# Storing split projection weights in the mixer's first block, and moving one PSUM copy from VectorE to ScalarE

## The chip, the cores and the metric

The kernel runs on one core of one Trainium2 chip. The metric is the device time of one execution in microseconds; three runs of the kernel before gave 3564.45, 3571.49 and 3570.65 us, median 3570.65. Engines are named as in the profile: PE is TensorE, DVE is VectorE, ACT is ScalarE, POOL is GpSimd, SP is SyncE. On SP only DMA issues run in this kernel, and all DMAs of it are issued there.

## The reference: what is computed

One encoder layer over 2048 tokens of width 1024: a hybrid token mixer (half mLSTM with 4 heads, half RWKV7 with 8 heads), cross attention to 256 memory rows, and a gated FFN with a short convolution. The change lies in the mixer. What it computes, shortened:

```python
def hybrid_token_mixer(h, w_in, ...):
    p = h @ w_in                       # 1024 x 3880 columns
    pm, pr = p[..., :M_COLS], p[..., M_COLS:]
    qk = silu(causal_dwconv(pm[..., :2 * M_WIDTH], m_conv_w, m_conv_b))
    hm = mlstm_chunkwise(q, k, v, i_pre, f_pre)
    y_m = sigmoid(o) * standardize_heads(hm) * m_norm_g
    pr = token_shift(pr, r_mu)
    ...
    yr = rwkv7_scan(rr, w, kr, vr, kk, a)
    ...
    return concatenate([y_m, y_r], -1) @ w_out

def rwkv7_scan(r, w, k, v, kk, a):
    def step(state, inp):
        sk = einsum('bhvk,bhk->bhv', state, kk_t)
        state = (state * w_t[:, :, None, :] - sk[..., None] * (kk_t * a_t)[:, :, None, :]
                 + v_t[..., None] * k_t[:, :, None, :])
        return state, einsum('bhvk,bhk->bhv', state, r_t)
```

All of it is in float32, and the result is compared with the float32 reference.

## The kernel before

**Split matmuls.** A float32 matrix product is made of three matmuls in the type fp32r: a number is split into a high part (a cast to fp32r) and a low part (the number minus its high part), and hi·hi + hi·lo + lo·hi are accumulated. An activation tile `hA` (128 x 2 x 512) holds both parts of 128 features by 512 tokens. A weight (128 output columns by 1024 inputs, 512 KB) is loaded as one tile `wraw` (`load_raw`, line 96; two buffers) and split in two halves q = 0, 1 of four 128x128 tiles each: ACT casts (`whi`, line 101), POOL subtracts (`wlo`, line 105; in the mixer every twelfth on DVE). `whi` and `wlo` have four buffers each, two weights. A projection (`proj`, `dense_g`, line 122) is 24 matmuls of 128x128 by 512.

**The mixer** goes over the tokens in four blocks of 512. In each block the stream `st_dense` makes 31 projections with the 31 weight groups of `w_in`: number 14 first, then 12 and 13 (`block_front`), then in turn three for a pair of RWKV heads (`f`) and four for an mLSTM head (`q`, in `qkvo`). So each of the 31 weights is loaded and split once a block, four times in all (124 loads of `wraw<-w_in`). At a block's begin `norm_block` builds the eight `hA` tiles: DVE scales (362), ACT casts (363), and line 364 subtracts for the low part, on DVE where k is odd and on POOL where it is even. `hA` has eight buffers, one block. `proj` of number 14 takes the low parts of the activations last (`late`).

**The other streams** of the mixer: `rwkv_pre` prepares a pair of heads and stores blocks of its triangular matrices (`nd<-F`, line 642), `rwkv_solve` inverts 16x16 blocks on DVE after a round trip through DRAM (656, 676, 678), `rwkv_merge` joins them, `rwkv_seq` goes through the eight chunks of 64 tokens in order, and `rwkv_tail`, `gates`, `mlstm` and `mlstm_tail` do the rest. `norm_stats` loads the next block's tokens (`xtok`).

**One chunk of `rwkv_seq`**, which the change touches: PE makes `qy` from state and `UV`; after LQ (1241 ns of planned time) ACT copies `qy` to `q` (747), ACT scales the old state to `sp` (749), PE multiplies the solved matrix with `q` into `pu`; the 64 solved rows are copied from PSUM into `UV` (755, on DVE); after LU (178 ns) PE makes `pS` from `UV`, DVE the new state `sbd` (761), PE the chunk's output, which ACT copies to `yt` (768). There are 16 pairs of heads and blocks with eight chunks each, 128 in all.

**What sets the order.** Each stream is a Python generator; `run_streams` interleaves them by a planned clock that counts PE time alone and the latencies (LQ, LU, ...) given after each step, with the fixed priority seq, gates, tail, merge, ml, pre, dense. That gives the order in which instructions are written. The framework's scheduler then sets each engine's queue from that order, by its own simulation, buffers included; every engine works through its queue in order. After the four blocks `kv_prep` makes the attention's folded key and value weights, and then attention and FFN follow, which use `load_w` too (w_out, f_up).

Of the kernel before, what the change touches and what calls it, by code (L numbers as in the profile page):

```python
# [56 lines left out]
def tile_hybrid_encoder(ctx: ExitStack, tc: tile.TileContext, t_in: dict, out: bass.AP, stage: str = "all"):  # L57
# [50 lines left out]
    wld = [12]  # L108
    wn = [0]

    def load_w(src):
        raw = load_raw(src)
        return [split_w(raw[:, 4 * q:4 * q + 4, :], [P, 4, P], wpool, ("whi", "wlo"), WB) for q in range(2)]

    pe = [0.0]
    DG = 1
# [126 lines left out]
    def mixer():  # L243
# [36 lines left out]
        LB, LPW, LPA, LSS, LPB, LKR, LPV = 3718, 2651, 17094, 3221, 2104, 1813, 344  # L280
        LF, LG, LGD, LQK, LFD, LME, LM1 = 1590, 0, 1147, 3611, 844, 676, 3063
        LM2, LM3, LM4, LMD, LSOLVE = 2779, 438, 1685, 295, 39163
        LATE, PRB, HD, TSB = True, 2, 1, 6
        PMG = PM

        def norm_stats(tok0):
# [61 lines left out]
        def norm_block(tok0, st):  # L348
            rs, xs = st
            bc = PD(name="bc")  # L350
            for j in range(4):
                mm(bc[:, j * P:(j + 1) * P], rs[:, j:j + 1].to_broadcast([P, P]), ident, start=True, stop=True)
            yield LB
            hs = []
            for k in range(KT):
                h = kt.tile([P, 2, TB], FR, tag="kt", name="hA")
                if xs:
                    xr = xs[k]
                else:
                    xr = T(name="xraw")  # L360
                    nc.sync.dma_start(xr, t_in["xT"][k * P:(k + 1) * P, tok0:tok0 + TB])
                nc.vector.scalar_tensor_tensor(xr, xr, V("norm_mix", k), bc, ALU.mult, ALU.mult)
                nc.scalar.copy(h[:, 0, :], xr)  # L363
                (nc.vector if k % 2 and (xs or HD) else nc.gpsimd).tensor_tensor(h[:, 1, :], xr, h[:, 0, :].bitcast(F32), ALU.subtract)
                hs.append(h)
            return hs

        w14 = load_w(t_in["w_in"][14])
        rs = norm_stats_first()


# [358 lines left out]
        def rwkv_seq(d):  # L730
            j, pc = d["j"], d["pc"]
            yt = TS((P, 4, P), "yt")
            for cg in range(NC_):
                sd_, c = d["subs"][cg // 4], cg % 4
                KR, F, UV = sd_["KR"], sd_["F"], sd_["UV"]
                sb, sn = sbd[j][scount[j] % 2], sbd[j][(scount[j] + 1) % 2]
                scount[j] += 1
                qy = PY((P, P), "qy")
                mm(qy, KR[:, c, :], sb, start=True, stop=False, skip_group_check=True)
                for h in range(2):  # L740
                    hs = slice(h * 64, h * 64 + 64)
                    g = 2 * c + h
                    mm(qy[0:66, hs], F[:, g * 130:g * 130 + 66], UV[:, c, hs], start=False, stop=True,
                                     skip_group_check=True)
                yield LQ
                q = sm.tile([P, P], F32, name="q")
                nc.scalar.copy(q, qy)
                sp = sm.tile([P, P], F32, name="sp")
                nc.scalar.activation(sp, sb, AF.Copy, scale=pc[:, cg:cg + 1])
                pu = PU((P, P), "pu")  # L750
                for h in range(2):
                    hs = slice(h * 64, h * 64 + 64)
                    g = 2 * c + h
                    mm(pu[0:66, hs], sd_["R"][:, g * 64:g * 64 + 66], q[:, hs], start=True, stop=True)
                nc.vector.tensor_copy(UV[0:64, c, :], pu[0:64])
                yield LU
                pS = PU((P, P), "pS")
                mm(pS, sd_["et"][c // 2][:, c % 2, :], UV[:, c, :], start=True, stop=True)
                for h in range(2):
                    hs = slice(h * 64, h * 64 + 64)  # L760
                    nc.vector.scalar_tensor_tensor(sn[hs, hs], pS[hs, hs], pc[hs, cg:cg + 1], sp[hs, hs], ALU.mult, ALU.add)
                for h in range(2):
                    hs = slice(h * 64, h * 64 + 64)
                    g = 2 * c + h
                    mm(qy[:, hs], F[:, g * 130 + 2:g * 130 + 130], UV[:, c, hs], start=False, stop=True,
                                     skip_group_check=True)
                o = (cg % 2) * 64
                nc.scalar.copy(yt[o:o + 64, cg // 2, :], qy[64:128])
                if c == 3:
                    yield ("set", "seq_sub")  # L770
                yield LS
            return yt
# [152 lines left out]
        def block_front(blk, w14, rs):  # L925
            h_ = hraw if U0 and blk == 0 else (yield from norm_block(blk * TB, rs))
            x14 = shift((yield from proj(w14, h_, LATE)), 14)
            s1f = x14[0:32]
            nc.scalar.activation(s1f, s1f, AF.Tanh, scale=0.5)
            nc.vector.tensor_scalar(s1f, s1f, 0.5, 0.5, ALU.mult, ALU.add)  # L930
            s1 = lp.tile([96, TB], FR, name="sg1", bufs=2)
            nc.scalar.copy(s1[0:32], s1f)
            nc.scalar.copy(s1[64:96], s1f)
            nc.vector.tensor_tensor(s1[32:64], s1f, s1[0:32].bitcast(F32), ALU.subtract)
            bks[blk] = dict(h=h_, x14=x14, tok0=blk * TB)
            yield ("set", ("x14", blk))
            x12 = shift((yield from proj(load_w(t_in["w_in"][12]), h_)), 12)
            thf = x12[0:64]
            nc.scalar.activation(thf, thf, AF.Tanh)
            tw_ = lp.tile([P, TB], FR, name="tw_")  # L940
            nc.scalar.copy(tw_[0:64], thf)
            nc.vector.tensor_tensor(tw_[64:128], thf, tw_[0:64].bitcast(F32), ALU.subtract)
            ta_ = lp.tile([P, TB], FR, name="ta_")
            nc.scalar.copy(ta_[64:128], x12[64:128])
            nc.vector.tensor_tensor(ta_[0:64], x12[64:128], ta_[64:128].bitcast(F32), ALU.subtract)
            x13 = shift((yield from proj(load_w(t_in["w_in"][13]), h_)), 13)
            sg0 = lp.tile([P, TB], F32, name="sg0", bufs=2)
            nc.scalar.activation(sg0, x13, AF.Tanh, scale=0.5)
            nc.vector.tensor_scalar(sg0, sg0, 0.5, 0.5, ALU.mult, ALU.add)
            bks[blk]["lora"] = (tw_, ta_, sg0, s1)  # L950

        def qkvo(bk, h):
            q2 = conv_qk((yield from proj(load_w(t_in["w_in"][15 + 4 * h]), bk["h"], conv=True)), h)
            k2 = conv_qk((yield from proj(load_w(t_in["w_in"][16 + 4 * h]), bk["h"], conv=True)), 4 + h)
            xv = TM(name="mv")
            nc.scalar.copy(xv, (yield from proj(load_w(t_in["w_in"][17 + 4 * h]), bk["h"], conv=True)))
            og = TM(name="og")
            nc.scalar.activation(og, (yield from proj(load_w(t_in["w_in"][18 + 4 * h]), bk["h"], conv=True)), AF.Tanh, scale=0.5)
            nc.vector.tensor_scalar(og, og, 1.0, mngh[:, h:h + 1], ALU.add, ALU.mult)
            return q2, k2, xv, og  # L960

# [4 lines left out]
        def st_dense():  # L966
            rs_ = rs
            for b in range(NBLK):
                if b == 0:
                    yield from block_front(b, w14, rs_)  # L970
                else:
                    yield from block_front(b, load_w(t_in["w_in"][14]), rs_)
                if b + 1 < NBLK:
                    rs_ = norm_stats((b + 1) * TB)
                nf, nq = 4 * b, 4 * b
                for what in (DL if b + 1 == NBLK else DO):
                    if what == "f":
                        i, j, nf = nf, nf % 4, nf + 1
                        if i > 0:
                            yield ("wait", ("pre", i - 1) if W1 == 0 else ("presub", i - 1, 1), 0)  # L980
                        xs = []
                        for which in range(3):
                            xs.append(shift((yield from proj(load_w(t_in["w_in"][3 * j + which]), bks[b]["h"])), which * 4 + j))
                        fr[i] = xs
                        yield ("set", ("fd", i))
                    else:
                        i, j, nq = nq, nq % 4, nq + 1
                        if i > 0:
                            yield ("wait", ("ml_mid" if W2 < 2 else "pht", i - 1), 0)
                            if W2 == 0:  # L990
                                yield ("wait", ("pht", i - 2), 0)
                        qk[i] = yield from qkvo(bks[b], j)
                        yield ("set", ("qk", i))
# [487 lines left out]
```

## Time and profile before

| | before |
|---|---|
| median of 3 runs | 3570.65 us (3564.45 to 3571.49) |
| the profiled execution | 3564.44 us, span 3562.6 us |
| granted PE clock, mean | 0.981 |
| busy: PE, DVE, ACT, POOL | 3377.6, 2020.6, 1256.2, 1368.7 us |
| `whi` casts (line 101), all | 383.4 us in 596 |
| `wlo` subtractions on POOL (line 105), all | 785.7 us in 544 |
| DMA | 342.01 MB, mean 96 GB/s |

How its lines are read: a group of instructions names line, engine, operation, output and inputs, the count, then busy time and mean ns of one, then the engine's idle time just before them with what ended it. A line of waits names who waited, for whom, the total in us, how often, and the longest. A row of stretches gives for each engine its busy time and, in brackets, its instructions. "min/median/max" rows give durations in ns. Waits are inferred from semaphores; idle time of an engine that does not set the end costs nothing.

### The profile page before, as it was taken

The page shows a single profiled execution, that of the slowest core. Times are in us where ns is not written, and L with a number is a line of the kernel's source. Part 1 is how long each engine was busy: PE and PEld are TensorE (multiplying, and loading weights), DVE is VectorE, ACT ScalarE, POOL GpSimd, SP SyncE. Part 2 cuts the span into 40 slices and gives each one's busy share as a digit, 9 for nine tenths or more (in the row PEclk, how much of TensorE's full clock was granted, in tenths as well). Part 3 has the DMA queues.
Part 4 walks back from the last instruction along what each step waited for, and adds up shares of the span by engine and source line. Part 5 has one row for each costly group of instructions (what it writes and reads, how often), then busy time and mean ns, then how long its engine had stood idle before and what let it go on. Part 6 is the DMA issues. An engine that isn't in the chain of part 4 may idle for free.

```text
span 3562.6 us, 48272 instructions
## 1 busy us (share of the span) xinstructions
PE 3377.6 (95%) x17836; PEld 2750.2 (77%) x17836; DVE 2020.6 (57%) x4038; ACT 1256.2 (35%) x2397; POOL 1368.7 (38%) x1364
## 2 busy tenths in 40 slices
PE   7999999999989999789999999999999999999997
PEld 5777777777767778668888888888788888888886
DVE  6788888878888887433333343444453344344345
ACT  5345434544454444433222212212442222222213
POOL 5233333433333322353144434434632343443433
PEclk9999999999999999899999999999999999999998
DMA  4223222322222234685621111112566411111111
GB/s 131 80 67 111 77 72 75 111 70 68 90 73 69 73 94 146 212 269 177 222 71 43 59 42 54 54 36 71 154 219 212 141 55 36 54 54 42 54 48 54
DMA packets 203388, 342.01 MB, mean 96 GB/s; under 512 B 77072, under 2 KB 108944, under 8 KB 203152
## 3 DMA queue, kind: packets, MB, share of 16 engines
q1 hardware_dynamic: 203152, 338.92, 30.2%
q8 instruction: 141, 2.31, 0.3%
q14 instruction: 95, 0.78, 0.1%
HBM read 293.68 MB, written 45.15 MB: 95 GB/s over the span
## 4 chain that ended last, share of the span: by engine, by line
PE 55%; DMA 4%; DVE 2%; ACT 1%; issue 0%; POOL 0%; SPq 0%; DVEq 0%; ACTq 0%; POOLq 0%
PE pd L148 11%; PE pd L151 11%; PE pd L150 11%; PE dps L1354 4%; PE dps L1352 4%; PE dps L1353 4%; DMA x<-xT 2%; PE sc L1233 1%; PE sc L1235 1%; PE sc L1234 1%; DVE x L1369 0%; DMA wqk<-qk_dram 0%; PE ppt L1258 0%; DVE x L1201 0%; DMA y<-y_dram 0%
## 5 line engine op out<-in xcount | busy, mean ns | idle before, releaser
L105 POOL TENSOR_TENSOR wlo<-wraw,whi 128x512 fp32r<-128x512 f32 (+1 forms) x544 | 785.7, 1451 | 813.0 <-ACT whi L101 736.3
L122 PE MATMUL pd<-hA,whi 128*128 128x512 f32 x1984 | 677.6, 415 | 11.2 <-ACT uconv L824 5.8
L101 ACT CAST whi<-wraw 128x512 fp32r<-128x512 f32 (+1 forms) x596 | 383.4, 651 | 540.9 <-PE pd L150 222.0
L151 PE MATMUL pd<-h,wlo 128*128 128x512 f32 x1408 | 547.9, 389 | 0.0
L148 PE MATMUL pd<-h,whi 128*128 128x512 f32 x1408 | 547.9, 389 | 0.0
L150 PE MATMUL pd<-h,whi 128*128 128x512 f32 x1408 | 547.7, 389 | 0.0
L122 PEld LDWEIGHTS pd<-hA,whi 128*128 128x128 f32 x1984 | 357.5, 191 | 80.4 <-ACT hA L363 8.3
L122 PE MATMUL pd<-hA,wlo 128*128 128x512 f32 x992 | 402.2, 405 | 0.0
L1355 DVE TENSOR_TENSOR x<-dps,x 128x512 f32<-128x512 f32 x352 | 235.5, 689 | 224.3 <-PE dps L1354 222.2
L150 PEld LDWEIGHTS pd<-h,whi 128*128 128x128 f32 x1408 | 264.3, 188 | 54.8
L151 PEld LDWEIGHTS pd<-h,wlo 128*128 128x128 f32 x1408 | 264.3, 188 | 54.8
L148 PEld LDWEIGHTS pd<-h,whi 128*128 128x128 f32 x1408 | 264.3, 188 | 54.7
L1354 PE MATMUL dps<-act,wlo 128*128 128x512 f32 x704 | 271.5, 390 | 0.0
L1353 PE MATMUL dps<-act,whi 128*128 128x512 f32 x704 | 271.4, 390 | 0.0
L1352 PE MATMUL dps<-act,whi 128*128 128x512 f32 x704 | 261.6, 390 | 3.2 <-DVE x L1355 2.6
L122 PEld LDWEIGHTS pd<-hA,wlo 128*128 128x128 f32 x992 | 189.8, 191 | 34.2 <-issue 0.7
L1336 DVE SCALAR_TENSOR_TENSOR fu<-fu,pd 128x512 f32<-128x512 f32 x88 | 60.5, 688 | 226.6 <-PE pd L151 221.7
L1155 POOL TENSOR_TENSOR sq<-sq 128x512 f32<-128x512 f32 x56 | 73.9, 1320 | 252.9 <-ACT sq L1152 231.5
L1352 PEld LDWEIGHTS dps<-act,whi 128*128 128x128 f32 x704 | 132.6, 188 | 31.9 <-DVE x L1355 3.4
L1354 PEld LDWEIGHTS dps<-act,wlo 128*128 128x128 f32 x704 | 132.6, 188 | 27.6
L1353 PEld LDWEIGHTS dps<-act,whi 128*128 128x128 f32 x704 | 132.4, 188 | 27.5
L1330 POOL TENSOR_TENSOR fu<-fu,bcs 128x512 f32<-128x512 f32 x88 | 114.2, 1298 | 97.1 <-DVE fu L1329 95.6
(913 smaller groups left out, 6220.2 us busy)
## 6 DMA issues: line engine op xcount, KB each, us to landing
wraw<-w_in SPq DMA_DIRECT2D x124, 512.0 KB, 3.5
wraw<-f_up SPq DMA_DIRECT2D x88, 512.0 KB, 3.4
wqk<-qk_dram SPq DMA_DIRECT2D x64, 512.0 KB, 5.3
wvo<-vo_dram SPq DMA_DIRECT2D x64, 512.0 KB, 4.2
wraw<-f_down SPq DMA_DIRECT2D x44, 512.0 KB, 3.4
wraw<-w_out SPq DMA_DIRECT2D x32, 512.0 KB, 5.6
y<-y_dram SPq DMA_DIRECT2D x32, 256.0 KB, 7.0
x<-xT SPq DMA_DIRECT2D x32, 256.0 KB, 5.1
```

What stands on the lines that cost most here:

```text
L101: nc.scalar.copy(hi, raw)
L105: (nc.vector if dve else nc.gpsimd).tensor_tensor(lo, raw, hi.bitcast(F32), ALU.subtract)
L122: nc.tensor.matmul(out_, lhsT, rhs, **kw)
L148: nc.tensor.matmul(ps, hi[:, k % 4, :], a[:, 0, :n], start=(k == 0), stop=False)
L150: nc.tensor.matmul(ps, hi[:, k % 4, :], a[:, 1, :n], start=False, stop=False)
L151: nc.tensor.matmul(ps, lo[:, k % 4, :], a[:, 0, :n], start=False, stop=(k == last and not late))
L1155: (nc.vector if fast else nc.gpsimd).tensor_tensor(acc, acc, sq, ALU.add)
L1330: nc.gpsimd.tensor_tensor(u, u, bc3[b], ALU.mult)
L1352: nc.tensor.matmul(ps, hi[:, d, :], a[:, 0, :], start=(g == 0), stop=False)
L1353: nc.tensor.matmul(ps, hi[:, d, :], a[:, 1, :], start=False, stop=False)
L1354: nc.tensor.matmul(ps, lo[:, d, :], a[:, 0, :], start=False, stop=(g == GRP - 1))
L1355: nc.vector.tensor_tensor(xs[b][d], ps, xs[b][d], ALU.add)
```

## The change

Three things:

1. A weight's halves become one tile each with high and low part (`halves`: 128 x 2 x 4 x 128, tag `whl`, four buffers; the same bytes as `whi` and `wlo` had). In block 0 `load_in` loads and splits as before and stores each half in a DRAM tensor `w_split` as soon as both parts are there, on the same SP queue. In blocks 1 to 3 it loads the two stored halves, 512 KB each, straight into `whl`: no `wraw`, no cast, no subtraction. `load_w` without `keep` serves kv_prep, attention and FFN.
2. `HD` is gone: after block 0 (no `xs`) line 364 runs on POOL for every k.
3. The solved rows (line 755) are copied by ACT in place of DVE.

```diff
@@ load_w
-    def load_w(src):
+    def halves():
+        return [wpool.tile([P, 2, 4, P], FR, tag="whl", name="whl", bufs=WB) for _ in range(2)]
+
+    def load_w(src, keep=None):
         raw = load_raw(src)
-        return [split_w(raw[:, 4 * q:4 * q + 4, :], [P, 4, P], wpool, ("whi", "wlo"), WB) for q in range(2)]
+        w = halves()
+        for q, t_ in enumerate(w):
+            r_ = raw[:, 4 * q:4 * q + 4, :]
+            nc.scalar.copy(t_[:, 0], r_)
+            wn[0] += 1
+            dve = wn[0] % wld[0] == 0 if wld[0] else False
+            (nc.vector if dve else nc.gpsimd).tensor_tensor(t_[:, 1], r_, t_[:, 0].bitcast(F32), ALU.subtract)
+            if keep is not None:
+                WQ.dma_start(keep[q], t_.bitcast(F32))
+        return [(t_[:, 0], t_[:, 1]) for t_ in w]
+
+    w_split = dram.tile([NWIN, 2, P, 2, 4, P], F32, name="w_split")
+
+    def load_in(n, blk):
+
+        if blk == 0:
+            return load_w(t_in["w_in"][n], w_split[n])
+        w = halves()
+        for q, t_ in enumerate(w):
+            WQ.dma_start(t_.bitcast(F32), w_split[n, q])
+        return [(t_[:, 0], t_[:, 1]) for t_ in w]
@@ norm_block
-                (nc.vector if k % 2 and (xs or HD) else nc.gpsimd).tensor_tensor(h[:, 1, :], xr, h[:, 0, :].bitcast(F32), ALU.subtract)
+                (nc.vector if k % 2 and xs else nc.gpsimd).tensor_tensor(h[:, 1, :], xr, h[:, 0, :].bitcast(F32), ALU.subtract)
@@ rwkv_seq
-                nc.vector.tensor_copy(UV[0:64, c, :], pu[0:64])
+                nc.scalar.copy(UV[0:64, c, :], pu[0:64])
@@ block_front, qkvo, st_dense: every load_w(t_in["w_in"][n]) of the mixer
-            x12 = shift((yield from proj(load_w(t_in["w_in"][12]), h_)), 12)
+            x12 = shift((yield from proj(load_in(12, blk), h_)), 12)
...
-                            xs.append(shift((yield from proj(load_w(t_in["w_in"][3 * j + which]), bks[b]["h"])), which * 4 + j))
+                            xs.append(shift((yield from proj(load_in(3 * j + which, b), bks[b]["h"])), which * 4 + j))
```

More of the change, by code (lines that the diff above doesn't have):

```diff
@@ L282, in mixer @@
         LM2, LM3, LM4, LMD, LSOLVE = 2779, 438, 1685, 295, 39163
-        LATE, PRB, HD, TSB = True, 2, 1, 6
+        LATE, PRB, TSB = True, 2, 6
         PMG = PM
@@ L363, in norm_block @@
                 nc.scalar.copy(h[:, 0, :], xr)
-                (nc.vector if k % 2 and (xs or HD) else nc.gpsimd).tensor_tensor(h[:, 1, :], xr, h[:, 0, :].bitcast(F32), ALU.subtract)
+                (nc.vector if k % 2 and xs else nc.gpsimd).tensor_tensor(h[:, 1, :], xr, h[:, 0, :].bitcast(F32), ALU.subtract)
                 hs.append(h)
             return hs
-        w14 = load_w(t_in["w_in"][14])
+        w14 = load_in(14, 0)
         rs = norm_stats_first()
@@ L945, in block_front @@
             nc.vector.tensor_tensor(ta_[0:64], x12[64:128], ta_[64:128].bitcast(F32), ALU.subtract)
-            x13 = shift((yield from proj(load_w(t_in["w_in"][13]), h_)), 13)
+            x13 = shift((yield from proj(load_in(13, blk), h_)), 13)
             sg0 = lp.tile([P, TB], F32, name="sg0", bufs=2)
@@ L952, in qkvo @@
         def qkvo(bk, h):
-            q2 = conv_qk((yield from proj(load_w(t_in["w_in"][15 + 4 * h]), bk["h"], conv=True)), h)
-            k2 = conv_qk((yield from proj(load_w(t_in["w_in"][16 + 4 * h]), bk["h"], conv=True)), 4 + h)
+            q2 = conv_qk((yield from proj(load_in(15 + 4 * h, bk["tok0"] // TB), bk["h"], conv=True)), h)
+            k2 = conv_qk((yield from proj(load_in(16 + 4 * h, bk["tok0"] // TB), bk["h"], conv=True)), 4 + h)
             xv = TM(name="mv")
-            nc.scalar.copy(xv, (yield from proj(load_w(t_in["w_in"][17 + 4 * h]), bk["h"], conv=True)))
+            nc.scalar.copy(xv, (yield from proj(load_in(17 + 4 * h, bk["tok0"] // TB), bk["h"], conv=True)))
             og = TM(name="og")
-            nc.scalar.activation(og, (yield from proj(load_w(t_in["w_in"][18 + 4 * h]), bk["h"], conv=True)), AF.Tanh, scale=0.5)
+            nc.scalar.activation(og, (yield from proj(load_in(18 + 4 * h, bk["tok0"] // TB), bk["h"], conv=True)), AF.Tanh, scale=0.5)
             nc.vector.tensor_scalar(og, og, 1.0, mngh[:, h:h + 1], ALU.add, ALU.mult)
@@ L971, in st_dense @@
                 else:
-                    yield from block_front(b, load_w(t_in["w_in"][14]), rs_)
+                    yield from block_front(b, load_in(14, b), rs_)
                 if b + 1 < NBLK:
```

## The prediction

> **What bounds the kernel now.** I began with the page, then took stretches of the span, then asked who keeps TensorE (PE) waiting, then who keeps those engines.
>
> ```profile
> span 3562.6 us, 48272 instructions
> ...
> PE   7999999999989999789999999999999999999997
> ...
> DVE  6788888878888887433333343444453344344345
> ```
>
> PE is the bound from end to end, and the first 15 slices (89 us each) are another machine than the rest: there VectorE (DVE) is at 80%, later at 30 to 40%. That is the mixer. The change touches hardly anything behind it, so the question is what PE loses inside it. The mixer by stretches; the columns are length, busy time of PE, PE weight loads, DVE, ACT (ScalarE) and POOL (GpSimd), then clock, DMA share and GB/s:
>
> ```profile
> 50.00:310.00 260.00, 237.15 (x1415) 188.58 (x1414) 206.45 (x494) 111.07 (x231) 87.69 (x103) 0.97 0.27 80
> 310.00:645.00 335.00, 311.18 (x2072) 244.40 (x2072) 278.39 (x689) 156.37 (x335) 116.27 (x136) 0.99 0.28 86
> 645.00:980.00 335.00, 312.95 (x2039) 246.14 (x2038) 274.52 (x689) 156.23 (x331) 118.93 (x134) 0.97 0.28 82
> 980.00:1320.00 340.00, 315.63 (x2080) 247.95 (x2078) 279.13 (x690) 156.13 (x327) 114.81 (x132) 0.97 0.26 76
> ...
> 1450.00:1560.00 110.00, 83.35 (x414) 67.80 (x415) 44.07 (x49) 43.47 (x80) 43.89 (x33) 0.88 0.74 240
> ```
>
> Block 0 runs to about 310, blocks 1 to 3 from there to 1320. PE idles 22.9 us in the first and 23.8 + 22.1 + 24.4 = 70.2 us in the others: 93 us is all that can be won, apart from clock. Who ended that idle time, blocks 1 to 3 first, block 0 second:
>
> ```profile
> PE pS L122 <- DVE UV L755: 30.1, 34, 2.2
> PE qy L122 <- DVE sbd L761: 11.7, 18, 2.0
> PE gtr L126 <- ACT xs L515: 10.2, 3, 5.3
> PE pv L126 <- DVE n L580: 4.2, 4, 2.0
> PE pw L122 <- DVE tw__7382 L942: 2.5, 1, 2.5
> ```
> ```profile
> PE pS L122 <- DVE UV L755: 9.4, 7, 2.7
> ```
>
> The largest item is exactly the copy that the change moves: 39.5 us. No weight (whi, wlo) is on the list: weights are never late today.
>
> **Part 1, the UV copy from DVE to ACT.** The copy (line 755), a copy of the same 64x128 shape from PSUM that ACT already makes (768), and who waits for ACT's copy q one step earlier in the chain (747):
>
> ```profile
> L755 DVE COPY UV<-pu x128: 247/283/285, 183.7 to 1420.1; 64x128 f32<-64x128 f32 x128
> ```
> ```profile
> L768 ACT COPY yt<-qy x128: 261/262/265, 184.9 to 1421.3; 64x128 f32<-64x128 f32 x128
> ```
> ```profile
>   PEld pu L122: 15.4, 48
> ...
>   PE pu L122: 0.6, 1
> ```
>
> The copy itself gains 21 ns, nothing. The gain is in the queue: DVE is busy 832.0 of 1010 us (82%) in blocks 1 to 3, ACT 468.7 (46%). Bounds: 39.5 us if nothing of the wait is left, 0 if ACT is as late as DVE. The q row says that ACT holds PE up for 0.6 us in a like place, but the written order leaves 1241 ns ahead of that step (LQ) and only 178 ahead of this one (LU). ACT also stands still while it waits in order (below). I leave a third: **-26 us**.
>
> **Part 2, what blocks 1 to 3 no longer compute.** Casts on ACT, low halves on POOL and DVE, and the two-operand DVE work beside them:
>
> ```profile
> L101 ACT CAST whi<-wraw 128x512 fp32r<-128x512 f32 x187 | 114.8, 617 | 149.7 <-PE pd L122 120.0 <-issue 18.1 <-POOL F L626 4.4
> ```
> ```profile
> L105 POOL TENSOR_TENSOR wlo<-wraw,whi 128x512 fp32r<-128x512 f32 x171 | 239.0, 1400 | 390.6 <-ACT whi L101 329.7 <-PE pd L122 12.3 <-DVE UV L755 8.2
> L364 POOL TENSOR_TENSOR hA<-xraw,hA 128x512 fp32r<-128x512 f32 x12 | 17.9, 1500 | 11.2 <-ACT hA L363 11.2
> ```
> ```profile
> L755 DVE COPY UV<-pu 64x128 f32<-64x128 f32 x96 | 26.8, 280 | 22.3 <-PE pu L122 20.4
> L788 DVE TENSOR_TENSOR yt<-yt,gnvr 128x512 f32<-128x512 f32 x13 | 20.7, 1593 | 22.9 <-POOL gnvr L158 22.9
> L612 DVE SCALAR_TENSOR_TENSOR KR<-xs,vec,Pt 128x256 f32<-128x256 f32 x24 | 16.6, 691 | 0.9 <-ACT Pt L553 0.6 <-PE qy L122 0.2
> L364 DVE TENSOR_TENSOR hA<-xraw,hA 128x512 fp32r<-128x512 f32 x12 | 12.5, 1043 | 1.2 <-ACT hA L363 1.1
> L105 DVE TENSOR_TENSOR wlo<-wraw,whi 128x512 fp32r<-128x512 f32 x16 | 12.0, 750 | 1.7 <-ACT whi L101 1.6
> ```
> ```profile
> L788 DVE TENSOR_TENSOR yt<-yt,gnvr x16: 691/1748/1776, 230.7 to 1429.7; 128x512 f32<-128x512 f32 x16
> ```
> ```profile
> L612 DVE SCALAR_TENSOR_TENSOR KR<-xs,vec,Pt x32: 466/480/1515, 74.3 to 1309.7; 128x256 f32<-128x256 f32 x32
> ```
>
> And the timeline of one moment (start, length):
>
> ```profile
> 291.82 1.74 POOL L105 TENSOR_TENSOR wlo<-wraw,whi 128x512 fp32r<-128x512 f32 x1 [4.10 <-ACT whi L101]
> ...
> 292.33 1.78 DVE L569 SCALAR_TENSOR_TENSOR ta<-ta,pinv 128x512 f32<-128x512 f32 x1
> ```
>
> ACT loses 114.8 us of casts and, with them, 120.0 us in which it stood in order until PE freed a weight slot; it gains 96 x 0.262 = 25.2 us of copies: 468.7 - 114.8 + 25.2 = 379 us, 38%. DVE loses 26.8 (UV), 12.5 (line 364, to POOL) and 12.0 (its share of low halves): 51.3 us. It also loses contention: the same instruction takes 691 or 1776 ns (788), 466 or 1515 ns (612), and in the timeline such a long one (1.78 us) runs beside a low half on POOL, itself stretched to 1.74. Over their shortest, these two groups lose 13 x 0.902 + 24 x 0.225 = 17 us; that is the lower bound, and 171 x 1.05 = 180 us, every POOL subtraction hitting one DVE instruction, the upper. I take 40, since most DVE groups have a PSUM operand or small tiles. DVE: 832 - 51 - 40 = 741 us, 73%.
>
> For waits on DVE other than UV (11.7 + 4.2 + 2.5 = 18.4 quoted) I scale the queue as u/(1-u): 0.82/0.18 = 4.6 becomes 0.73/0.27 = 2.7, 41% less: **-8 us** (bounds 0 and -18). The gates (gtr, 10.2 us) hang on ACT and DVE at block changes: **-4 us** (bounds 0 and -10).
>
> **Clock.** Short and long idle times of PE differ in what follows them:
>
> ```profile
> 510.00:515.00 5.00, 3.08 (x20) 2.33 (x19) 3.75 (x10) 0.50 (x3) 2.04 (x3) 1.00 0.33 120
> ...
> 1015.00:1020.00 5.00, 0.00 (x1) 0.00 (x0) 4.91 (x9) 2.11 (x4) 3.42 (x3) 0.77 0.33 110
> 1020.00:1025.00 5.00, 4.67 (x27) 4.25 (x28) 3.01 (x11) 2.04 (x6) 0.00 (x0) 0.50 0.35 105
> ```
>
> After 1.9 us idle the granted clock stays 1.00; after 5 us it is 0.50. The UV waits are at most 2.7 us, so they bring no clock back; only the gates do: **-4 us** (bounds 0 and -23, the 2.3% of 1010 us by which the mean clock is under 1). [...]
>
> **Part 3, transfers and SyncE (SP).** All DMAs are issued in order by SP. Block 0 adds 62 stores of 512 KB (32.5 MB); blocks 1 to 3 replace 93 loads by 186 of that size, 48.8 MB more.
>
> ```profile
> SPq L96 <- POOL wlo L105: 135.9, 26, 14.8
> ...
> SPq L642 <- DVE F L636: 78.9, 14, 15.0
> ```
> ```profile
> L96 SPq DMA_DIRECT2D wraw<-w_in x124: 327/351/745, 1.3 to 1286.1; - x124
> ...
> DMA to landing us min/median/max: 3.3/3.5/7.5
> ```
> ```profile
> L122 PE MATMUL pd<-hA,whi x1984: 387/393/796, 21.3 to 1318.3; 128*128 128x512 f32 x199
> ```
>
> Bandwidth: 32.5 MB over 260 us is 125 GB/s on top of 80, 205; the stretch at 1450 moves 240 at a share of 0.74. Later 48.8 MB over 1010 us is 48 on top of 82. It fits. Issue: 62 + 93 more at 0.35 us are 54 us on SP, which spends far more than that waiting.
>
> A store waits on SP until POOL has its low half; behind it stand the next raw loads and the nd, rd and y transfers. But the next raw load waits for that same subtraction today (135.9 us), so the hold is not new. Bounds 0 and, if every one of block 0's 31 loads took 7.5 instead of 3.5 us unhidden, 124; two raw buffers hide it: **+3 us**.
>
> The new wait is that of a piece: it may not be issued before PE has read the old contents of its half. Halves come free 1.5 weights ahead of their use, 36 x 0.393 = 14.1 us (16 at the real pace of 1010/93 = 10.9 us a weight). Landing takes 3.5, so 10.6 us are left. Before, raw and split tiles together held four weights ahead. Behind the waiting piece stand nd stores, which the solve on DVE needs; those wait up to 15.0 us on SP themselves. Bounds 0 and the second rival: **+6 us**.
>
> Line 364: eight low halves on POOL at 1.50 us end 0.6 + 12.0 us after the first cast, where PE with its low terms last (late) wants the eighth after about 23 x 0.393 = 9.0 us. Up to 3.6 us late at each of three block changes, 11 at worst, 0 where other streams fill: **+2 us**. In the attention and FFN stages a slot of the joint tile comes free one matmul later (0.39 us of a 9.4 us weight) under a full PE: 0; without that cover it would be 0.39 us for each of 120 loads, 47.
>
> **Sum.** -26 - 8 - 4 - 4 + 3 + 6 + 2 = -31 us. The profiled execution took 3564.4 us around its span of 3562.6; it is the fastest of three, 6.2 under their median of 3570.65. 3564.4 - 31 = 3533, 3570.65 - 31 = 3540; I say **3536 us**.
>
> **Rivals.**
>
> *ACT becomes as late as DVE was* (3564). ACT is in order, and it waits long for others:
>
> ```profile
> ACT yt L768 <- PE qy L122: 119.4, 72, 4.5
> ...
> ACT thc L829 <- DVE uconv L826: 21.4, 11, 5.8
> ```
>
> A UV copy behind thc waits for DVE all the same. If all 39.5 us stay, the sum is -8 - 4 - 2 (clock) + 11 = -3: 3561 to 3568. For it: the LU of 178 ns. Against it: 0.6 us for q.
>
> *Pieces come late behind SP* (3590, slower). One mechanism: a piece stands behind an nd store that waits for F on DVE. It decides from holds over 10.6 us. If all 14 holds reached the longest, each weight would be 15.0 - 10.6 = 4.4 us late, 62 us; with the gains but without the +6: 3564 - 37 + 62 = 3589. For it: all in one queue, half the depth. Against it: their mean is 78.9/14 = 5.6 us, and DVE gets faster.
>
> *The relief feeds itself* (3498): no wait for UV (-39.5), two thirds off DVE's others (-12) and the gates (-7), clock -10, costs +3: -66. For it: DVE, ACT and POOL all get lighter at once. Against: an order written for other loads.
>
> **Chances.** Forecast 0.60 (by itself 3515 to 3555), ACT late 0.17, pieces late 0.13, more relief 0.10. About 0.2% (7 us) is what can be told from no change, 3563.5 to 3577.8. Faster: 0.58 + 0.10 + half of ACT late, 0.08 = 0.76; same: 0.02 + 0.09 = 0.11; slower: 0.13. The range runs from just above the third rival to the end of the first, 3500 to 3577; the slower rival and some of the third are left out.
>
> **What would show it.** Right: PE's wait for UV under 15 us with ACT named, DVE near 73% and ACT near 38% in blocks 1 to 3, PE idle there 35 to 45 us instead of 70. The shortest and longest of 612 close together after block 0. Wrong: pd waiting for a DMA of pieces (second rival), pS waiting for ACT as long as now (first), or new idle time of PE in block 0, which would be the stores.

## The result, and the profile after

| | before | changed |
|---|---|---|
| median | 3567.55 us (3564.34 to 3571.49, 4 runs) | 3481.44 us (3477.47 to 3488.72, 4 runs) |
| profiled execution | 3564.44 us, span 3562.6 | 3488.72 us, span 3486.9 |

The ratio is 0.976 with a 95% interval of 0.974 to 0.9781: 86 us faster. The forecast was 3536, with a range that began at 3500; even the rival with more relief (3498) is passed. The direction was right, the size was not.

The page of the changed kernel, the rows that were shown of before:

```profile
span 3486.9 us, 47820 instructions
...
PE   6899999999999998799999999999999999999997
...
DVE  5877777777776785344244444444553344444445
```

The mixer is shorter by about one slice, and DVE stands at 7 tenths in it where it stood at 8. Block 1's first cast (line 363, 386 in the changed kernel) starts at 313 us before and at 322 after, and the last projection of block 3 ends at 1318 and at 1255. By stretches between these points (length, then busy time of PE, PE loads, DVE, ACT, POOL; clock, DMA share, GB/s), before:

```profile
21.00:313.00 292.00, 266.73 (x1548) 211.35 (x1548) 228.43 (x522) 133.96 (x269) 109.59 (x123) 0.96 0.28 85
...
313.00:1318.00 1005.00, 934.76 (x6123) 734.17 (x6122) 827.17 (x2059) 466.11 (x987) 346.46 (x398) 0.98 0.27 80
```

and after:

```profile
21.00:322.00 301.00, 270.08 (x1547) 211.66 (x1548) 222.82 (x507) 135.76 (x284) 103.63 (x117) 0.95 0.54 190
...
322.00:1255.00 933.00, 917.95 (x6129) 734.62 (x6127) 692.86 (x1937) 384.89 (x902) 124.94 (x243) 0.99 0.44 138
```

Block 0 became 9 us longer, blocks 1 to 3 became 72 us shorter. Of the 72, PE's idle time is 55 (1005 - 934.76 = 70.2 to 933 - 917.95 = 15.1), and 17 are in PE's busy time for the same 6120 or so matmuls, at a mean clock of 0.99 in place of 0.98. Behind the mixer lie another 13 us (2244.6 to 2231.9 from there to the end of the span). 9 - 72 - 13 = -76, the difference of the two profiles. The medians differ by 86, because the profile of before is of its fastest execution but one and that of the changed kernel of its slowest; every account by stages below explains 76 us.

What PE still waits for in blocks 1 to 3, after:

```profile
PE qy L145 <- DVE sbd L784: 7.1, 15, 1.3
PE pS L145 <- ACT UV L778: 5.1, 4, 1.8
PE pn L145 <- DVE e L889: 0.9, 1, 0.9
```

The UV copy's wait went from 30.1 to 5.1 us, sbd from 11.7 to 7.1, and the gates (10.2) and the small ones are gone. No wait for a transfer is among them. What SP waited for in the same stretch:

```profile
SPq L135 <- PE pd L145: 262.6, 106, 10.7
...
SPq L665 <- DVE F L659: 64.1, 11, 10.5
```

The pieces do stand at the head of SP's queue until PE frees a half, 106 times, and the longest hold is 10.7 us. The prediction's slower rival needed nd stores that wait for F for more than 10.6 us, with a piece behind them; the longest of the 11 is 10.5 us, just below, and nothing came late. The transfers themselves land as quickly as the raw loads did (3.5 us before), the stores quicker; the raw loads of block 0 now take 5.2 us beside them (KB each, median us to landing):

```profile
whl<-w_split SPq DMA_DIRECT2D x186, 512.0 KB, 3.4
...
w_split<-whl SPq DMA_DIRECT2D x62, 512.0 KB, 2.6
...
wraw<-w_in SPq DMA_DIRECT2D x31, 512.0 KB, 5.2
```

Last, the group that the prediction named as the sign of contention, line 612 before, 635 now (shortest, median, longest in ns; 466/480/1515 before):

```profile
L635 DVE SCALAR_TENSOR_TENSOR KR<-xs,vec,Pt x32: 474/480/486, 81.0 to 1243.4; 128x256 f32<-128x256 f32 x32
```

Not one of its 32 instructions is stretched any more. Of the other groups, blocks 1 to 3, those that read PSUM had not been stretched (`xs<-pd` 743 ns before, 748 after), while small tiles had been; a group with two SBUF inputs of 64x1, before and after:

```profile
L656 DVE TENSOR_TENSOR pr<-ru,nu 64x1 f32<-64x1 f32 x12 | 4.9, 406 | 0.7 <-DMA nu<-nd 0.7
```
```profile
L679 DVE TENSOR_TENSOR pr<-ru,nu 64x1 f32<-64x1 f32 x12 | 1.7, 145 | 2.1 <-DMA nu<-nd 2.0
```

### The profile page after: what moved, and what is told of

It is laid out like the page before. It is cut to its first block, busy times and chain, and to the rows that moved or that the text cites. A ratio compares the mean times of both kernels' runs of the same rounds, so it can differ in the third digit from the quotient of the medians.

```text
span 3486.9 us, 47820 instructions
## 1 busy us (share of the span) xinstructions
PE 3355.8 (96%) x17836; PEld 2747.0 (79%) x17836; DVE 1899.4 (54%) x3883; ACT 1177.4 (34%) x2339; POOL 1137.9 (33%) x1205
## 4 chain that ended last, share of the span: by engine, by line
PE 80%; DVE 8%; DMA 4%; issue 3%; ACT 2%; POOL 2%; SPq 1%; DVEq 0%; POOLq 0%; ACTq 0%
PE pd L145 13%; PE pd L174 12%; PE pd L171 12%; PE pd L173 12%; PE dps L1377 4%; PE dps L1376 4%; PE dps L1375 4%; PE qy L145 2%; PE sc L1256 2%; PE sc L1258 2%; PE sc L1257 2%; PE pab L145 1%; DVE pr L679 1%; DVE pr L699 1%; PE p L145 1%
## 5 line engine op out<-in xcount | busy, mean ns | idle before, releaser
L145 PE MATMUL pd<-hA,whl 128*128 128x512 f32 x2976 | 818.2, 411 | 14.1 <-ACT whl L119 7.4
L145 PEld LDWEIGHTS pd<-hA,whl 128*128 128x128 f32 x2976 | 530.4, 191 | 119.0 <-ACT whl L119 9.2
L122 POOL TENSOR_TENSOR whl<-wraw,whl 128x512 fp32r<-128x512 f32 x329 | 439.2, 1346 | 380.4 <-ACT whl L119 346.2
L174 PE MATMUL pd<-h,whl 128*128 128x512 f32 x1408 | 547.9, 389 | 0.0
L171 PE MATMUL pd<-h,whl 128*128 128x512 f32 x1408 | 547.9, 389 | 0.0
L173 PE MATMUL pd<-h,whl 128*128 128x512 f32 x1408 | 547.7, 389 | 0.0
L119 ACT CAST whl<-wraw 128x512 fp32r<-128x512 f32 x366 | 222.6, 621 | 332.9 <-PE pd L174 268.4
L173 PEld LDWEIGHTS pd<-h,whl 128*128 128x128 f32 x1408 | 264.3, 188 | 54.8
L174 PEld LDWEIGHTS pd<-h,whl 128*128 128x128 f32 x1408 | 264.3, 188 | 54.8
L171 PEld LDWEIGHTS pd<-h,whl 128*128 128x128 f32 x1408 | 264.3, 188 | 54.8
L1352 DVE SCALAR_TENSOR_TENSOR fu<-fth,fu 128x512 f32<-128x512 f32 x88 | 87.9, 999 | 67.6 <-ACT fth L1351 67.6
L145 PE MATMUL qy<-UV,F 128*66 128x64 f32 (+1 forms) x1024 | 123.5, 243 | 0.0
```

Source lines behind the costliest of these rows:

```text
L119: nc.scalar.copy(t_[:, 0], r_)
L122: (nc.vector if dve else nc.gpsimd).tensor_tensor(t_[:, 1], r_, t_[:, 0].bitcast(F32), ALU.subtract)
L145: nc.tensor.matmul(out_, lhsT, rhs, **kw)
L171: nc.tensor.matmul(ps, hi[:, k % 4, :], a[:, 0, :n], start=(k == 0), stop=False)
L173: nc.tensor.matmul(ps, hi[:, k % 4, :], a[:, 1, :n], start=False, stop=False)
L174: nc.tensor.matmul(ps, lo[:, k % 4, :], a[:, 0, :n], start=False, stop=(k == last and not late))
```

## The experiments

Two theories of the 86 us were put against each other. *Copy*: PE waited for the UV copy behind DVE's queue, so moving it is the gain. *Relief*: DVE was slowed by GpSimd's subtractions, and the copy was only where that showed. Times of before in these series: medians of 3566.0 to 3567.75 us.

### The UV copy alone

```diff
-                nc.vector.tensor_copy(UV[0:64, c, :], pu[0:64])
+                nc.scalar.copy(UV[0:64, c, :], pu[0:64])
```

> Only the copy of the solved rows moves from VectorE to ScalarE; weights are split in every block as before. Two theories of the 86 us. Copy: what TensorE waited for was this one copy behind VectorE's queue, so moving it alone gives most, 45 us or more (below 3522). Relief: VectorE is slowed and filled by GpSimd's subtractions, and the copy was only the place where it showed; then moving it gives about its own wait, 20 to 30 us (3537 to 3547), the copy's wait falls from 39.5 to under 15 us, and the other waits for VectorE (sbd, n, e) stay or grow.

3558.02 us, ratio 0.9976 (0.9961 to 0.999): 9 us. PE's waits from 50 to 1308 us:

```profile
PE qy L122 <- DVE sbd L761: 43.7, 46, 2.8
PE pS L122 <- ACT UV L755: 8.5, 6, 4.0
```

The copy's wait fell as expected, from 39.5 to 8.5. But the next link of the same chain, the new state sbd, which is still made on DVE, rose from 11.9 us in all of the mixer to 43.7. The wait moved one step on: 31 us of it were taken away and 32 came back. The copy theory is wrong, and so is the prediction's -26 for this part. The relief theory had expected too much as well, 20 to 30 us for the copy alone, though it said that sbd could grow.

### The stored pieces alone

The changed kernel with the UV copy on VectorE and line 364 alternating as before.

> Block 0 stores the split weights and blocks 1 to 3 load them; the copy stays on VectorE and line 364 alternates as before. Copy theory: 20 us at most (3547 or more), the copy's wait of 30 us in blocks 1 to 3 stays. Relief theory: 45 to 60 us (3507 to 3522), the copy's wait in blocks 1 to 3 falls under 15 us although it is still on VectorE, and VectorE is near 76% busy there instead of 82%.

3487.91 us, ratio 0.9777 (0.9755 to 0.9798): 80 of the 86 us. Blocks 1 to 3:

```profile
318.00:1249.00 931.00, 913.10 (x6128) 732.11 (x6127) 721.71 (x2043) 365.05 (x807) 110.53 (x231) 1.00 0.45 138
```

PE idles 17.9 us here, nearly as little as with the whole change, though DVE is busy for 29 us more than there. DVE's work as such is not what PE paid for. From 50 to 1255 us PE waits for the UV copy, still on DVE:

```profile
PE pS L145 <- DVE UV L778: 14.2, 21, 2.7
```

It is 14.2 us in place of 39.5, 7.5 of them in blocks 1 to 3 in place of 30.1, with the same copy on the same engine. That is under 15, as the relief theory expected, and the gain is more than it expected (45 to 60). DVE is busy for 78% of blocks 1 to 3 (76 expected).

### Line 364 alone

```diff
-                (nc.vector if k % 2 and (xs or HD) else nc.gpsimd).tensor_tensor(...)
+                (nc.vector if k % 2 and xs else nc.gpsimd).tensor_tensor(...)
```

> Only line 364 goes to GpSimd for every k after block 0; 12 subtractions in all. Both theories: within 7 us of before. Copy theory: 0, the 12.5 us of VectorE do not matter. Relief theory: 0 to +5 us, since GpSimd is still crowded with weights here and its reads hold VectorE up.

3569.17 us, ratio 1.0004 (0.9992 to 1.0017): nothing, as both had it.

### GpSimd's subtractions put back

```diff
+        d_ = wpool.tile([P, 8, P], F32, tag="wraw", name="dum", bufs=2)
         for q, t_ in enumerate(w):
             WQ.dma_start(t_.bitcast(F32), w_split[n, q])
+            nc.gpsimd.tensor_tensor(d_[:, 4 * q:4 * q + 4, :], t_[:, 0].bitcast(F32), t_[:, 1].bitcast(F32), ALU.subtract)
```

> The changed kernel, and in blocks 1 to 3 GpSimd subtracts once more for each loaded half, 186 subtractions of 128x512 into a scratch tile that nobody reads. Output unchanged. VectorE gets its contention back, not its work, nor ScalarE its casts. Relief theory: 25 to 50 us of the gain go (3506 to 3531), VectorE's line 635 (612 before) is again over 600 ns on the mean. Copy theory: under 10 us (below 3491).

3579.98 us, ratio 1.0034 (1.002 to 1.0047). The whole gain is gone, and 12 us with it: 98 us for 186 subtractions that nobody waits for by data, twice to four times what the relief theory expected (25 to 50). Blocks 1 to 3:

```profile
326.00:1349.00 1023.00, 949.84 (x6129) 750.87 (x6128) 801.32 (x1935) 387.72 (x903) 374.98 (x427) 0.96 0.41 126
```

DVE executes the same 1935 instructions as in the changed kernel (1937), and is busy 801 instead of 693 us. PE idles 73 instead of 15, its busy time grows by 32 and its clock falls to 0.96. The KR group is at 635 ns on the mean of the 20 instructions between 330 and 1250 us (480 in the changed kernel). A group that shows it better, the taps of the convolution (two SBUF inputs; line 826 and 817 ns before the change), in the changed kernel and here:

```profile
L849 DVE SCALAR_TENSOR_TENSOR uconv<-qc,vec,uconv 128x512 f32<-128x512 f32 x72 | 53.7, 747 | 2.2 <-ACT uconv L847 1.9
```
```profile
L851 DVE SCALAR_TENSOR_TENSOR uconv<-qc,vec,uconv 128x512 f32<-128x512 f32 x69 | 70.9, 1028 | 0.8 <-ACT uconv L849 0.6
```

747 against 1028 ns: the extra subtractions stretch this group more than the kernel before did. PE waits again for what DVE makes, with the UV copy on ScalarE and all:

```profile
PE qy L147 <- DVE sbd L786: 32.6, 33, 2.5
PE pS L147 <- ACT UV L780: 11.7, 9, 3.1
PE pv L151 <- DVE n L605: 8.5, 2, 4.2
PE pd L147 <- POOL hA L389: 5.7, 8, 1.7
```

The extra subtraction also holds the half's slot and keeps GpSimd's own queue busy, and might act by these. The next two take that apart.

### A reader more on ScalarE

```diff
+            nc.scalar.copy(d_[:, 4 * q:4 * q + 4, :], t_[:, 0].bitcast(F32))
```

> The changed kernel, and in blocks 1 to 3 ScalarE casts the high part of each loaded half once more into a scratch tile, 186 casts of 128x512. As with the extra subtractions a reader holds the half's slot and an engine has its old load back, but ScalarE's reads do not touch VectorE's. If what counts is VectorE's contention with GpSimd: within 12 us of the changed kernel (3475 to 3495). If the slot held by one reader more, or the casts on ScalarE, made the kernel before slow: 25 us or more are lost (3506 or more).

3487.52 us, ratio 0.9773 (0.9749 to 0.9798). 186 casts more on ScalarE (485.6 us busy instead of 384.9 in blocks 1 to 3), each holding the slot, cost 6 us, within the spread of the runs. DVE is busy for 692.0 us beside them and for 692.9 in the changed kernel, and the taps of the convolution take 747 ns in both. Neither a slot held by one more reader nor the casts had made the kernel before slow.

### GpSimd busy without reading

```diff
+            for n_ in (8, 2):
+                tc.keep_in_program_order(nc.gpsimd.memset(d_[:, 0:n_, :], 0.0))
```

> The changed kernel, and for each loaded half GpSimd writes zeros over 128x1024 and 128x256 of a scratch tile, pinned behind what was written for GpSimd before: about 1.3 us of GpSimd time for each of 186 halves, as the extra subtraction took 1.29, but it reads nothing from SBUF and holds no slot. If the loss of the extra subtractions (98 us) came from reads that hold VectorE up: at most 20 us lost (3481 to 3502), line 635 stays near 480 ns. If it came from GpSimd's own queue being long: 60 us or more lost (3541 or more).

3504.88 us, ratio 0.9827 (0.9803 to 0.985): 23 us lost, 3 more than the contention theory allowed and far from the 60 of a long GpSimd queue. Blocks 1 to 3, and the same group:

```profile
322.00:1261.00 939.00, 918.53 (x6127) 735.90 (x6126) 704.37 (x1936) 383.91 (x900) 341.77 (x608) 0.99 0.44 137
```
```profile
L852 DVE SCALAR_TENSOR_TENSOR uconv<-qc,vec,uconv 128x512 f32<-128x512 f32 x70 | 52.3, 747 | 2.4 <-ACT uconv L850 2.1
```

GpSimd is busy for 342 us, close to the 375 of the subtractions, and this DVE group takes 747 ns as in the changed kernel, where GpSimd is busy for 125 us; KR stays at 481. The 11 us that DVE lost all the same lie mostly in instructions with one input (about 9 us of them between 330 and 1240 us), such as `sw<-sw` (128x512; 425 ns in the changed kernel, 615 here). Blocks 1 to 3 are 6 us longer than in the changed kernel; where the rest of the 23 us lies the two profiles, 11 us apart, do not show.

One difference is left between the two runs: a subtraction must wait until its piece has landed, and GpSimd stood 254.6 us at the head of its queue for that. What came of it is bounded by who waited for GpSimd. PE waited 5.7 us for its hA low halves and PE's weight loads 8.7, against none and 0.7 with the memsets; DVE waited 36 us, and 37 in the changed kernel. So about 75 of the 98 us, 98 - 23, come with subtractions and not with memsets; at most 14 of these by a late GpSimd, the others, as far as these two runs tell, by GpSimd reading SBUF while DVE works (the taps of the convolution: 1028 ns beside subtractions, 747 beside memsets).

### Half of the subtractions

```diff
+            if q == 0:
+                nc.gpsimd.tensor_tensor(d_[:, 0:4, :], t_[:, 0].bitcast(F32), t_[:, 1].bitcast(F32), ALU.subtract)
```

> The changed kernel with one extra subtraction a weight in blocks 1 to 3 in place of two: 93 instead of 186. If each subtraction costs its own stall of VectorE, half of the 98 us come back: 3525 to 3537. If it is a queue that gets long only where VectorE is nearly full, as the prediction's u/(1-u) has it, much less than half, under 35 us: below 3516.

3509.55 us, ratio 0.9846 (0.9804 to 0.9888). 28 us for the first 93 subtractions, 70 for the second 93, as the second expectation had it; half of the 98 us would have given 3531, and all four runs lie below (3506.98 to 3521.62). Blocks 1 to 3:

```profile
318.00:1269.00 951.00, 917.21 (x6125) 730.24 (x6124) 741.07 (x1934) 386.50 (x902) 249.88 (x335) 1.00 0.44 136
```

DVE's stretch is in proportion: 48 us for 93 (741 - 693) and 108 for 186, 0.52 and 0.58 us each. PE's idle time is not: 15.1, 33.8 and 73.2 us. And PE's busy time stays at 917 for the first half and is 950 at the full number, where the clock goes from 1.00 to 0.96. The loss grows faster than its cause, in two steps: PE's idle time grows at both doses, its busy time and clock change only at the full one.

### The stores, and the joint tile alone

Stores: the changed `load_w` with its stores in block 0, and raw loads and splits in every block; the joint tile: that without the stores. Both with the UV copy on VectorE and line 364 alternating.

```diff
     def load_in(n, blk):
         if blk == 0:
             return load_w(t_in["w_in"][n], w_split[n])
-        w = halves()
-        ...
+        return load_w(t_in["w_in"][n])
```

> Block 0 stores the split halves, and blocks 1 to 3 load and split the raw weights all the same; the copy stays on VectorE, line 364 alternates. Together with the joint tile this gives the price of the stores. From the two profiles block 0 is 9 us longer with them and what follows the mixer some 7 us shorter: 3560 to 3572. If the stores are free: 3553 to 3561. If they cost more than block 0 shows, over 3575.

> High and low part of a half share one tile, nothing else: no stores, no loads of pieces. In the two profiles the FFN stage is 7 us shorter after the change though nothing in it was meant to change. If the joint tile does that by another order of the same work: 3555 to 3562, the same 7 us in the same stage. If it is chance or comes from the mixer: 3564 to 3571.

Stores 3587.9 us (ratio 1.0063, 1.0038 to 1.0087), joint tile alone 3580.01 (1.0037, 1.0024 to 1.005): both worse than expected. The first is in its last case, over 3575, but 12 of its 20 us are the joint tile's. The stores cost 8 us by the medians, whose intervals overlap; the profiles put 9 us of it in block 0, where block 1's first cast starts at 319.1 us with them and at 309.9 without. The joint tile does shorten the FFN, as half of the guess had it; its projections ran so long before, with the joint tile alone, and after:

```profile
L148 PE MATMUL pd<-h,whi x1408: 387/389/478, 1805.3 to 3516.5; 128*128 128x512 f32 x176
```
```profile
L166 PE MATMUL pd<-h,whl x1408: 387/389/478, 1823.5 to 3529.1; 128*128 128x512 f32 x176
```
```profile
L171 PE MATMUL pd<-h,whl x1408: 387/389/478, 1735.6 to 3439.8; 128*128 128x512 f32 x176
```

1711.2, 1705.6 and 1704.2 us. Every profile with the joint tile has 1702 to 1707 us there and every one without it 1711 to 1715, so it is no chance; which order of the work does it was not looked for. But in blocks 1 to 3, where such tiles are split again, it costs 23 us:

```profile
310.00:1338.00 1028.00, 952.42 (x6106) 751.69 (x6106) 836.13 (x2057) 465.48 (x988) 343.31 (x397) 0.96 0.26 79
```

PE's idle time is 75.6 us and its clock 0.96. Why one tile in place of two does this to the mixer was not followed up. Against the run with tile and stores the pieces are worth 100 us (3587.9 to 3487.9); 20 of these only make up for what tile and stores cost, and 80 are left against the kernel before.

### Other places for the low halves

Three variants of the changed kernel: line 364 alternating again; on VectorE for every k in every block; and every third low half of block 0 on VectorE.

```diff
-                (nc.vector if k % 2 and xs else nc.gpsimd).tensor_tensor(...)
+                (nc.vector if k % 2 else nc.gpsimd).tensor_tensor(...)
...
+                nc.vector.tensor_tensor(...)
...
-    wld = [12]
+    wld = [3]
```

> The changed kernel with line 364 alternating between VectorE and GpSimd as before. Contention theory: 4 subtractions a block fewer on GpSimd against 2.8 us a block more on VectorE, so it is as fast or up to 6 us faster (3475 to 3482). If VectorE's work is what counts: 3 to 8 us slower (3484 to 3490). Together with the run of the pieces alone (3488) it separates the parts: this one differs from it by the ScalarE copy only.

> The changed kernel with line 386 (364 before) on VectorE for every k, block 0 too. Contention theory: GpSimd reads nothing at the block changes any more, 24 x 0.69 = 17 us more work on VectorE: 0 to 8 us faster (3473 to 3481). If VectorE's work counts: 5 to 15 us slower.

> The changed kernel with every third low half of block 0 on VectorE in place of every twelfth: 16 subtractions leave GpSimd, VectorE gets 16 x 0.69 = 11 us. By the price of the extra subtractions (98 us for 186, 0.53 us each) 8 us are won against at most 11 lost: 3476 to 3486, faster by the contention theory, slower if VectorE's work counts.

3484.86 (ratio 0.9772, 0.9748 to 0.9795), 3486.52 (0.9767, 0.9741 to 0.9792) and 3482.01 us (0.9754, 0.9729 to 0.9779), beside 0.976 of the change. None can be told from it or from each other. The first two medians lie in the range given for "VectorE's work counts", but by no more than the spread, so the expectations of a few us either way stay open: where a dozen or two subtractions run makes no difference that these runs can tell.

## Why the prediction was wrong

Its views led to the right place: PE is the bound, it loses 93 us in the mixer, the stored pieces take work and contention off DVE. The step that failed first is the price of contention, 40 us of DVE's time where 88 went, and with it the share of PE's waits that would go; the reading of the clock and the part of the copy failed too. By the two profiles, 76 us apart against 31 forecast: PE's idle time in blocks 1 to 3 fell by 55 (38 forecast for the UV copy, DVE's other waits and the gates), its busy time there by 17 (4 forecast as clock), block 0 grew by 9 (3 forecast), transfers and line 364 cost nothing (8 forecast), and 13 us came behind the mixer (0 forecast).

Some of the signs that the prediction gave for being right did come: PE's wait for UV fell to 5.1 us with ACT named, ACT is at 41% (38 forecast), DVE at 74% (73 forecast). The last is a coincidence: 741 of 1010 us was forecast, 693 of 933 was measured, and PE's idle time, 15 us against 35 to 45, shows the difference.

The terms of the sum, against what the runs showed:

- **The UV copy, -26.** It failed as a part of its own. Alone the change gives 9 us, because the wait passes to sbd. On top of the pieces, copy and line 364 together give 6 us (3487.9 to 3481.4), with overlapping intervals. In the changed kernel its wait did fall from 30.1 to 5.1 us in blocks 1 to 3, but without moving the copy the pieces bring it to 7.5. The step read a releaser in a list of waits as a cause that can be taken out.
- **Contention, 40 us of DVE's time, and u/(1-u), -8.** This is the term that decided, and both its parts were wrong. DVE's busy time fell by 827.2 - 692.9 = 134 us. Removed work at undisturbed length is 96 x 0.283 + 12 x 0.69 + 16 x 0.69 = 46 us (0.69 us is the shortest of line 788, the same shape), so contention was 88, twice the 40 taken from bounds of 17 and 180. Of the argument that most groups have a PSUM operand or small tiles, the first half holds (`xs<-pd`, 743 and 748 ns) and the second does not: the 64x1 group above went from 406 to 145 ns. And the scaling by mean load was the wrong law: the pieces alone leave DVE at 721.7 of 931 us, 78%, with 17.9 us of PE idle, the half dose at 741.1 of 951, also 78%, with 33.8, and the full dose at 801.3 of 1023, 78% again, with 73.2. At the same load, a queue with stretched instructions costs two and four times as much. That the loss grows faster than the number of subtractions was expected from this law and came out, but the load cannot be the reason. The runs suggest that what PE meets is the late moment of 1 us (line 788: 691 or 1776 ns), not the mean load; that was not shown instruction by instruction.
- **The gates, -4, and clock, -4.** The gates' 10.2 us went entirely, and PE's busy time fell by 17. The reading that only the gates' long waits cost clock was wrong already for the kernel before (stretches of 5 us; length, PE busy, clock, DMA share, GB/s):

```profile
565.00:570.00 5.00, 2.99 (x17) 0.71 0.33 107
...
825.00:830.00 5.00, 4.31 (x31) 0.66 0.50 141
830.00:835.00 5.00, 5.00 (x44) 0.66 0.21 85
```

In the first PE waited 2.0 us for DVE's n, in the second 0.7 us, and the clock fell in both; after a UV wait of 2.2 us at 1055 it fell to 0.87. So clock was lost beside short waits for DVE too, and its price should have grown with their relief. No run shows the term of -4: that waits of up to 2.7 us leave the clock alone was the author's estimate from waits of 1.9 and 5 us; in its place PE's busy time fell by 17 us, at a mean clock of 0.99 after 0.98. What else lowers the clock stays open: in the changed kernel it is 0.50 from 1107.5 to 1117.5 us with PE recorded as busy throughout.
- **Stores, +3:** 9 us in block 0 by the profiles, 8 by the stores' own run. **Pieces on SP, +6**, and **line 364, +2:** nothing to be seen, no wait of PE for a transfer, and no change that can be told for line 364 alone.
- **The FFN, 0:** 7 us shorter, 6 of them with the joint tile alone. That the slot that comes free a matmul later costs nothing was right; that the joint tile would gain there was not thought of. The other 6 us behind the mixer lie ahead of the FFN and were not looked into.

Of the rivals, that ACT becomes as late as DVE had something of the copy alone, a wait that stays, with the wrong engine: DVE's next instruction, not ACT. The third rival, relief that feeds itself, came nearest and was given 0.10; of its three engines DVE and GpSimd count, while ACT's casts put back cost nothing that can be told. It was priced at -66 by thinning the same list of waits; the profiles show -55 of idle and -17 of busy time in blocks 1 to 3, and -13 behind them. The range's lower end rested on that price.

## What to carry to other kernels

A list of waits names who came last, not what made it late: before costing the removal of one, look at the next instruction of the same chain on the busy engine: here 31 us of wait left the copy and 32 came back there. Compare the shortest and the mean duration of an engine's groups first; where they differ, as 466 and 691 ns here, ask whether another engine stretches them, and do not leave small tiles out. Taking that engine's work away can be worth more than the busy time that it frees on the list: here 88 us of stretch went beside 46 us of work. On PE, idle for 15 of 933 us, the loss grew faster than its cause here (28 us, then 70 for the same number of subtractions), so a relief should not be scaled by mean load. And before a term for the clock is left small, look at the clock after the short waits too (0.50 after one of 2.0 us here).

## What the runs showed of the hardware

GpSimd subtractions of 128x512 from SBUF made DVE 0.52 to 0.58 us slower each, in instructions that depend on them in no way; GpSimd memsets of nearly the same total time (GpSimd busy 342 and 375 us) added 11 us to DVE's busy time against 108. The stretch is mostly in instructions with two SBUF inputs (about 85 of 94 us between 330 and 1240 us, with all 186 subtractions), small ones too (128x512: 747 to 1028 ns; 64x1: 145 ns without the weights' subtractions, 406 with them), and not in `xs<-pd`, which reads PSUM (748 and 747 ns). The price in kernel time was 98 us for 186 x 1.29 = 240 us of such work on an engine that is otherwise 13% busy there (125 of 933 us). Loads of 97.5 MB in place of 48.8 in blocks 1 to 3 kept PE from nothing, and 32.5 MB of stores in block 0 came with 9 us there. The granted clock of PE fell to half also after a wait of 2.0 us (0.50 from 567.5 to 570 us of the kernel before), and in the changed kernel stood at 0.50 for 10 us without a recorded wait (1107.5 to 1117.5 us).
